# When the first tokens, the later tokens and the second block of weights are made ready at the start of a one-layer model

## The chip, the cores and the metric

The kernel runs on one core of a Trainium2 chip. The metric is device time in microseconds (us) of one execution. The profile speaks of the core's engines by short names: PE (TensorE, matrix products and transposes, with PEld for its weight loads), ACT (ScalarE), DVE (VectorE), POOL (GpSimd) and SP (SyncE, which issues most transfers). Each engine works through its own list of instructions in order.

## The reference

The reference is one layer of a hybrid model for 512 tokens of width 1024, in float32. It has a token mixer, an attention to a memory of 256 rows, and a mixture of 32 experts, each followed by a layer norm. Only the start of the token mixer matters here:

```
proj = h @ w_in                       # 512 x 1024 by 1024 x 8744
g_q, g_k, g_v, g_z, g_b, g_a, ... = split(proj)
qkv = silu(causal_dwconv(concat(g_q, g_k, g_v), conv_w))    # 4 taps
beta = sigmoid(g_b)
g = -exp(a_log) * softplus(g_a + dt_bias)
```

`g_z`, `g_b` and `g_a` lie side by side in `w_in`. `g` and `beta` are the gates of a delta rule that runs over chunks of 64 tokens. All outputs are needed in nearly float32 precision.

## The kernel before, in words

**Products in three parts.** A float32 operand is split into a high part (rounded, made by ACT) and a low part (the rest, made by DVE, from the high part); this is `split`, lines 137 to 139, and the text calls it *parting*. A product is then three matrix products (`mm3`, lines 222 to 224): weights high by tokens high, low, and crosswise. Both the tokens and every block of weights have to be parted first.

**Tokens.** `x` comes in four tiles of 128 tokens (t = 0 to 3, line 162). Since the products need tokens with the width on the partitions, `part(t)` (line 258) transposes a tile on PE in two groups of four (line 228) and parts each group out of PSUM.

**Blocks.** The wide product with `w_in` is cut into blocks of 256 or 260 columns. `dense` (line 179) goes through a list of them: it fetches the next block's raw weights as the present block begins, and writes the parting of the next block's weights into the program once a share `PART` (0.35) of the present block's estimated time is written. The first block is `z3` (line 335, columns of `g_z`, `g_b` and `g_a`): for each tile t it makes 24 products of 260 columns into a PSUM tile `mm`, DVE copies the gate columns out (`ab`, line 343), ACT takes a tanh (line 347) and DVE multiplies (`zl`, line 348). PSUM has two `mm` tiles, so a new group of products waits until the last reader of the group two before it, which is the line-348 step here, is done. The second block is called k00 here and the third k01: the key columns of heads 0 and 1, and of heads 2 and 3. Each is 48 products of 512 columns in two halves (c0 and c1), and after each half come a convolution (ACT line 432, three DVE steps of line 435), a tanh (ACT line 438), a multiplication (DVE line 439), and transposes on PE (line 228) that ACT copies out and squares (lines 469 and 471). The raw weights of k00 are parted in two pieces, those of k01 in one.

**Gates and sines.** After `z3`, `token_gates` (line 368) works out the gates in some twenty small DVE steps, up to `gg` (line 386), which PE then sums (lines 388 and 389). `rotary_sines` (line 295) takes two sines on ACT, which need another table of functions than tanh and exp do; `ACT_TABLE_LOAD` in the profile is such a change of tables.

**What sets the order.** A scheduling layer takes the program as written and lays down, ahead of time, a fixed order for each engine; buffers and waits follow from it. `tc.issue_after(i)` holds the instructions written in its block behind instruction i on i's engine. SP's order is that of the fetches.

Of the kernel before, what the change touches and what calls it, by code (L numbers as in the profile page):

```python
# [32 lines left out]
NT = S // 128  # L33
# [3 lines left out]
G_Q, G_K, G_V, G_Z, G_B = 0, 1024, 2048, 3072, 4096  # L37
N_Q, C_K, C_V, S_K, S_V, W_K, W_V, N_G, M_G = 4112, 5136, 5392, 5648, 5904, 6160, 6416, 6672, 6696
NBLK = 31
WB = 260  # L40
# [44 lines left out]
def body(tc, I, O, dbg=None):  # L85
    nc = tc.nc
    ctx = ExitStack()
    with ctx:
        _body(ctx, tc, nc, I, O, dbg or {})


def _body(ctx, tc, nc, I, O, dbg):
# [28 lines left out]
    def B8(shape, dt=FT):  # L121
        return big.tile(shape, dt, name="b8", bufs=NB8)

    def t512(shape, dt=FT):
        return wk.tile(shape, dt, name="t512", bufs=6)
# [5 lines left out]
    def rows_of(pr):  # L131
        return lambda t: pr[t // 2][:, t % 2]
# [4 lines left out]
    def split(hi, lo, src, eng=V):  # L137
        A.activation(hi, src, AF.Copy)  # L138
        eng.tensor_tensor(lo, src, hi.bitcast(FT), op=OP.subtract)  # L139

    def fetch_w(src, c0, n, loads=1):
        raw = B8([128, KD, WB])
        for k in pieces(loads):
            nc.sync.dma_start(raw[:, k, :n], src[128 * k.start:128 * k.stop, c0:c0 + n].rearrange("(k p) c -> p k c", p=128))
        return raw

    def load_w(src, c0, n, eng=V, loads=1, splits=1):
        return part_w(fetch_w(src, c0, n, loads), n, eng, splits)

    def part_w(raw, n, eng=V, splits=1):  # L150
        hi = B8([128, KD, WB], FR)
        lo = B8([128, KD, WB], FR)
        for k in pieces(splits):
            split(hi[:, k, :n], lo[:, k, :n], raw[:, k, :n], eng)
        return hi, lo

    def pieces(m):
        return [slice(KD // m * i, KD // m * (i + 1)) for i in range(m)]

    xn = [B8([128, 2, D]) for _ in range(2)]  # L160
    for t in range(NT):
        nc.sync.dma_start(xn[t // 2][:, t % 2], x_in[128 * t:128 * t + 128])
        if t == 0:
            first = load_w(I["w_in"][0], G_Z + 3 * WB, WB, loads=4, splits=4)

    bfm = ep.tile([128, 5, 128], BF, name="bfm")
    msk = t512([128, 512])
# [11 lines left out]
    def dense(blocks, cur=None):  # L179


        for j, b in enumerate(blocks):
            nb = blocks[j + 1] if j + 1 < len(blocks) else None
            raw, nxt, done = nb and fetch_w(*nb[1:4]), None, 0.0
            for us in b[4](*cur):
                yield us
                done += us
                if nb and nxt is None and done > PART * (5.3 if b[0][0] == "x" else 10.4):
                    nxt = part_w(raw, nb[3], splits=SPL.get(nb[0], 1))
            if nb and nxt is None:  # L190
                nxt = part_w(raw, nb[3])
            yield b[0]
            cur = nxt
# [26 lines left out]
    def mm3(out, wh, wl, xh, xl, first=True, last=True):  # L220

        T.matmul(out, wh, xh, start=first, stop=False)  # L222
        T.matmul(out, wh, xl, start=False, stop=False)  # L223
        T.matmul(out, wl, xh, start=False, stop=last)  # L224
# [29 lines left out]
    def parts_T(src):  # L254

        sh, sl = ([B8([128, 4, S], FR) for _ in range(2)] for _ in range(2))

        def part(t):
            for q in range(2):
                p = ps.tile([128, 512], FT, name="tp")  # L260
                transposes(p, [src(t)[:, (4 * q + i) * 128:(4 * q + i + 1) * 128] for i in range(4)])
                pv = p.rearrange("p (a b) -> p a b", a=4)
                split(sh[q][:, :, t * 128:(t + 1) * 128], sl[q][:, :, t * 128:(t + 1) * 128], pv)
        return sh, sl, part


    xh, xl, part = parts_T(rows_of(xn))
    for t in range(NT):
        part(t)


    ropec = ep.tile([128, S], FT, name="ropec")
# [2 lines left out]
    def before(engine):  # L275

        return [i for i in nc.cur_bb.bb.instructions if i.engine == engine][-1]
# [30 lines left out]
    p = ps.tile([128, 512], FT, name="tp")  # L308
# [5 lines left out]
    w_in = I["w_in"][0]  # L314

    def proj_tok(hi, lo, n, t, out):
        for k in range(KD):
            yield n * 3 / 2400
            mm3(out, xh[k // 4][:, k % 4, t * 128:(t + 1) * 128], xl[k // 4][:, k % 4, t * 128:(t + 1) * 128],
                hi[:, k, :n], lo[:, k, :n], first=k == 0, last=k == KD - 1)  # L320
# [14 lines left out]
    def z_block(j):  # L335

        def emit(hi, lo):
            n = WB if j < 3 else WB - 16
            for t in range(NT):
                p = ps.tile([128, 512], FT, name="mm")  # L340
                yield from proj_tok(hi, lo, WB, t, p[:, :WB])
                if j == 3:
                    V.tensor_copy(ab[:, t], p[:, n:WB])
                c = slice(WB * j, WB * j + n)
                zt = zl[:, t] if j == 3 else t512([128, WB])
                th = t512([128, WB])
                A.activation(th[:, :n], p[:, :n], AF.Tanh, scale=0.5)
                V.scalar_tensor_tensor(zt[:, :n], th[:, :n], 1.0, p[:, :n], op0=OP.add, op1=OP.mult)
                if j < 3:
                    m_ = rows_of(merged)(t)[:, c]  # L350
                    V.tensor_tensor(m_, m_, zt[:, :n], op=OP.mult)
        return ("z%d" % j, w_in, G_Z + WB * j, WB, emit)
# [698 lines left out]
    blocks += [{"m": m_block, "z": z_block}[b[0]](int(b[1])) for b in GATES]  # L1051
    blocks += [mem_block(j) for j in range(XB)] + [q_block(j) for j in range(4)] + [mem_block(j) for j in range(XB, 8)]
    W = Weave(dense(blocks, first))
    rotary()
    W.until("z3")
# [55 lines left out]
    for t in range(NT):  # L1111
        P = PP[t][:, 0].rearrange("p (a b) -> p a b", a=4)
        PT = PP[t][:, 1].rearrange("p (a b) -> p a b", a=8)
        for q in range(2):
            p = ps.tile([128, 512], FT, name="tp")
# [323 lines left out]
    def gate_up(pr, prev=None, last=False):  # L1439

        q, pp = pr // 2, pr % 2
        if not pp:
            rest = gather(q)
        xg = quads[q][0]
        if pr == 2:
            gb8.append(load_gb())
        load_next(6)
        ph = ps.tile([128, 512], FT, name="ga", bufs=4)
        hT = None
        for k in range(KD):  # L1450
            if pr == 0 and k == 4:
                rest()
            if prev is not None and k == (KB_LAST if last else KBACK):
                hT = swiglu(prev)
            if last and k == KD_LAST:
                down(pr - 1, hT)
            for i in range(2):
                T.matmul(ph[64 * i:64 * i + 64], xg[:, k, 128 * pp + 64 * i:128 * pp + 64 * i + 64],  # L1458
                         WT[2 * pr + i, k // 4][:, :, k % 4], start=k == 0, stop=k == KD - 1)
        if not pp:  # L1460
            if q == 0:
                weights()
            places(q)
        return ph, hT
# [21 lines left out]
    for pr in range(NE // 2 - 1):  # L1486
        last = pr == NE // 2 - 2
        nxt = gate_up(pr + 1, cur[0], last)
# [122 lines left out]
    with tc.If(most > CAP):  # L1611
# [5 lines left out]
        for t in range(NT):  # L1617
            for q in range(2):
                p = ps.tile([128, 512], FT, name="tp")
# [31 lines left out]
PART = 0.35  # L1651
# [22 lines left out]
```

## Time and profile before

| | us |
|---|---|
| median of 3 runs | 1229.37 (1223.86 to 1233.8) |
| the profiled execution, as timed | 1230.37 |
| its span, first to last instruction | 1228.4 |
| PE busy | 1162.4, 95% of the span |
| DVE busy | 655.3, 53% |
| ACT busy | 458.2, 37% |
| POOL busy | 133.6, 11% |
| mean granted clock of TensorE | 0.967 of full speed |

Times in the profile count from the start of the span. "Busy" is time in which an engine executes something. A row of the timeline gives when an instruction began, how long it took, and in brackets how long its engine had stood idle before it and what ended that wait. The chain of waits of this profile covers only the last two steps of the kernel and says nothing about the start, so the start has to be read from the timeline.

### The profile page before, as it was taken

The page shows a single profiled execution, that of the slowest core. Times are in us where ns is not written, and L with a number is a line of the kernel's source. Part 1 is how long each engine was busy: PE and PEld are TensorE (multiplying, and loading weights), DVE is VectorE, ACT ScalarE, POOL GpSimd, SP SyncE. Part 2 cuts the span into 40 slices and gives each one's busy share as a digit, 9 for nine tenths or more (in the row PEclk, how much of TensorE's full clock was granted, in tenths as well). Part 3 has the DMA queues.
Part 4 walks back from the last instruction along what each step waited for, and adds up shares of the span by engine and source line. Part 5 has one row for each costly group of instructions (what it writes and reads, how often), then busy time and mean ns, then how long its engine had stood idle before and what let it go on. Part 6 is the DMA issues. An engine that isn't in the chain of part 4 may idle for free. (4 is left out here: it accounts for less than half of the span.)

```text
span 1228.4 us, 20788 instructions
## 1 busy us (share of the span) xinstructions
PE 1162.4 (95%) x8356; PEld 926.7 (75%) x8356; DVE 655.3 (53%) x1667; ACT 458.2 (37%) x1093; POOL 133.6 (11%) x141
## 2 busy tenths in 40 slices
PE   6989999899999999999999899999989999999994
PEld 5887788678888789999998798889985445455532
DVE  4697377974865526556568667242583221221157
ACT  4643446444434124343356415244241111111224
POOL 4120000200000000000000101000020000000185
PEclk9998899898999999999999999999989999999997
DMA  8221112122222751212540614218447999999823
GB/s 273 69 69 37 35 35 69 35 71 69 70 69 83 236 156 59 71 36 69 206 125 14 196 52 138 66 52 293 172 172 262 329 381 371 406 398 386 318 84 130
DMA packets 101881, 189.21 MB, mean 154 GB/s; under 512 B 10246, under 2 KB 74438, under 8 KB 97680
## 3 DMA queue, kind: packets, MB, share of 16 engines
q1 hardware_dynamic: 93456, 181.58, 42.1%
q0 software_dynamic: 2224, 3.94, 1.0%
q10 hardware_dynamic: 6096, 2.27, 0.8%
q8 instruction: 68, 1.11, 0.4%
q14 instruction: 37, 0.30, 0.1%
HBM read 177.93 MB, written 13.63 MB: 156 GB/s over the span
## 5 line engine op out<-in xcount | busy, mean ns | idle before, releaser
L222 PE MATMUL mm<-b,b 128*128 128x256 f32 (+3 forms) x1216 | 403.7, 333 | 11.7 <-ACT b L138 7.7
L224 PE MATMUL mm<-b,b 128*128 128x256 f32 (+3 forms) x1216 | 392.8, 323 | 3.5 <-DVE b L139 3.5
L223 PE MATMUL mm<-b,b 128*128 128x256 f32 (+3 forms) x1216 | 392.4, 323 | 2.2 <-DVE b L139 2.2
L222 PEld LDWEIGHTS mm<-b,b 128*128 128x128 f32 x1216 | 232.6, 192 | 33.7 <-ACT b L138 8.5
L224 PEld LDWEIGHTS mm<-b,b 128*128 128x128 f32 x1216 | 232.7, 191 | 25.1 <-DVE b L139 4.2
L223 PEld LDWEIGHTS mm<-b,b 128*128 128x128 f32 x1216 | 233.2, 192 | 19.2 <-DVE b L139 3.0
L139 DVE TENSOR_TENSOR b<-b,b 128x2048 fp32r<-128x2048 f32 (+4 forms) x58 | 124.7, 2151 | 53.8 <-ACT b L138 43.6
L1458 PE MATMUL ga<-b,b 128*64 128x512 f32 x512 | 131.5, 608 | 6.8 <-DVE b L1345 6.8
L138 ACT ACTIVATE b<-b 128x2048 fp32r<-128x2048 f32 (+4 forms) x58 | 104.4, 1800 | 23.0 <-DMA b<-in_w_in_dram 5.8
L1458 PEld LDWEIGHTS ga<-b,b 128*64 128x64 f32 x512 | 38.4, 138 | 73.8 <-issue 63.2
L228 PE MATMUL tp<-cs,b 128*128 128x128 f32 x376 | 59.4, 285 | 11.1 <-DMA cs<-in_cst_dram 5.8
L435 DVE SCALAR_TENSOR_TENSOR t<-mm,cw,t 128x511 f32<-128x511 f32 (+2 forms) x72 | 53.7, 746 | 26.7 <-ACT t L432 25.4
L1473 PE MATMUL ga<-b,t 128*64 128x512 f32 x256 | 63.9, 593 | 0.5 <-ACT t L1317 0.5
L1338 PE MATMUL mm<-t,b 128*128 128x256 f32 x240 | 61.5, 294 | 0.0
L1310 DVE SCALAR_TENSOR_TENSOR t<-t,ga 128x256 f32<-128x256 f32 x16 | 6.7, 419 | 98.4 <-ACT t L1309 98.4
L228 PEld LDWEIGHTS tp<-cs,b 128*128 128x128 f32 x376 | 44.6, 146 | 17.6 <-DMA cs<-in_cst_dram 5.8
L1338 PEld LDWEIGHTS mm<-t,b 128*128 128x128 f32 x240 | 48.8, 204 | 0.8 <-issue 0.8
L1473 PEld LDWEIGHTS ga<-b,t 128*64 128x64 f32 x256 | 20.0, 137 | 36.2 <-issue 35.1
L1317 ACT ACTIVATE t<-tp 128x256 f32<-128x256 f32 x16 | 6.1, 383 | 88.8 <-PE tp L228 88.8
L826 POOL MEMSET b<- 128x97 f32 x32 | 5.4, 179 | 308.7 <-PE ga L773 204.3
L1321 POOL DMA_INDIRECT ybuf<-b,idx x14 | 13.7, 980 | 215.3 <-ACT b L1481 111.2
L1337 PE MATMUL mm<-t,hh 128*128 128x256 f32 x120 | 34.9, 311 | 0.0
(441 smaller groups left out, 1781.9 us busy)
## 6 DMA issues: line engine op xcount, KB each, us to landing
b<-in_moe_w_gate_dram SPq DMA_DIRECT2D x64, 512.0 KB, 10.6
b<-in_moe_w_up_dram SPq DMA_DIRECT2D x64, 512.0 KB, 10.4
b<-in_moe_w_down_dram SPq DMA_DIRECT2D x32, 1024.0 KB, 12.5
b<-in_w_in_dram SPq DMA_DIRECT2D x22, 1024.0 KB, 5.3
b<-in_w_in_dram SPq DMA_DIRECT2D x10, 1040.0 KB, 5.2
b<-in_cmp_w_dram SPq DMA_DIRECT2D x16, 512.0 KB, 7.4
b<-in_xa_wkv_dram SPq DMA_DIRECT2D x8, 1024.0 KB, 5.4
ybuf<-t SPq DMA_DIRECT2D x1, 4096.0 KB, 17.2
```

What stands on the lines that cost most here:

```text
L138: A.activation(hi, src, AF.Copy)
L139: eng.tensor_tensor(lo, src, hi.bitcast(FT), op=OP.subtract)
L222: T.matmul(out, wh, xh, start=first, stop=False)
L223: T.matmul(out, wh, xl, start=False, stop=False)
L224: T.matmul(out, wl, xh, start=False, stop=last)
L228: T.transpose(dst_psum[:, i * 128:(i + 1) * 128], s_, ident)
L435: V.scalar_tensor_tensor(acc[:, s_:], pp[:, :S - s_], cw[:, c_:c_ + 1], acc[:, s_:], op0=OP.mult, op1=OP.add)
L1321: G.indirect_dma_start(out=ybuf[:, :], out_offset=bass.IndirectOffsetOnAxis(ap=idx, axis=0), in_=yt, in_offset=None, bounds_check=2 * S - ...
L1337: T.matmul(p, rows_of(hh)(t)[:, c], sv, start=t == 0, stop=False)
L1338: T.matmul(p, rows_of(hl)(t)[:, c], sv, start=False, stop=t == NT - 1)
L1458: T.matmul(ph[64 * i:64 * i + 64], xg[:, k, 128 * pp + 64 * i:128 * pp + 64 * i + 64], WT[2 * pr + i, k // 4][:, :, k % 4], start=k == 0, ...
L1473: T.matmul(py[64 * i:64 * i + 64], hT[:, k, 64 * i:64 * i + 64], WT[2 * pr + i, 2][:, k, 512 * n:512 * n + 512], start=k == 0, stop=k == 1)
```

## The change

Four edits, all at the start of the program:

- the first block's raw weights are fetched at the same place as before, but parted later, after `part(0)`;
- only tile 0 of the tokens is transposed and parted ahead of block `z3`;
- `part(1)`, `part(2)` and `part(3)` are written inside `z3`, each after 15 of the 24 products of the tile before it (i counts the eight triples), and held behind the product written last on PE;
- within the first block alone, the parting of the second block's weights is written at a share of 0.8 of its time and not at 0.35.

```diff
     for t in range(NT):
         nc.sync.dma_start(xn[t // 2][:, t % 2], x_in[128 * t:128 * t + 128])
         if t == 0:
-            first = load_w(I["w_in"][0], G_Z + 3 * WB, WB, loads=4, splits=4)
+            first = fetch_w(I["w_in"][0], G_Z + 3 * WB, WB, loads=4)
...
-                if nb and nxt is None and done > PART * (5.3 if b[0][0] == "x" else 10.4):
+                if nb and nxt is None and done > (PART if j else 0.8) * (5.3 if b[0][0] == "x" else 10.4):
                     nxt = part_w(raw, nb[3], splits=SPL.get(nb[0], 1))
...
     xh, xl, part = parts_T(rows_of(xn))
-    for t in range(NT):
-        part(t)
+
+
+    part(0)
+    first = part_w(first, WB, splits=4)
...
                 p = ps.tile([128, 512], FT, name="mm")
-                yield from proj_tok(hi, lo, WB, t, p[:, :WB])
+                for i, us in enumerate(proj_tok(hi, lo, WB, t, p[:, :WB])):
+                    if j == 3 and i == 5 and t < NT - 1:
+                        with tc.issue_after(before(mybir.EngineType.PE)):
+                            part(t + 1)
+                    yield us
```

The changed file has two more lines from line 268 on, and six more from line 347 on, so that line 432 of before is line 438 there, 438 is 444 and so on. The text uses the numbers of before unless it says otherwise. SP's and POOL's orders are the same in both programs. On PE, ACT and DVE the order differs up to about an eighth of PE's list; behind that the three are the same.

**ScalarE, from its first parting into `z3`.** `b_83` are the first block's raw weights, `tp` a group of transposed tokens, `b_209` the raw weights of k00. Before:

```order
L138 ACTIVATE b_88<-b_83 128x520 x3
L138 ACTIVATE b_108<-tp 128x4x128
L138 ACTIVATE b_88<-b_83 128x520
L138 ACTIVATE b_109<-tp 128x4x128
L138 ACTIVATE b_108<-tp 128x4x128
L138 ACTIVATE b_109<-tp 128x4x128
L138 ACTIVATE b_108<-tp 128x4x128
L138 ACTIVATE b_109<-tp 128x4x128
L138 ACTIVATE b_108<-tp 128x4x128
L347 ACTIVATE t_237<-mm 128x244
L138 ACTIVATE b_109<-tp 128x4x128
L138 ACTIVATE b_250<-b_209 128x4x256
```

All four tiles of tokens stood ahead of the first piece of k00's weights. In the changed program, the same stretch (the raw weights of k00 are called `b_167` there):

```order
L138 ACTIVATE b_98<-tp 128x4x128
L138 ACTIVATE b_99<-tp 128x4x128
L138 ACTIVATE b_116<-b_83 128x520 x4
L313 ACTIVATE cw<-tp 128x96
L138 ACTIVATE b_98<-tp 128x4x128
L138 ACTIVATE b_99<-tp 128x4x128
L353 ACTIVATE t_209<-mm 128x244
L138 ACTIVATE b_302<-b_167 128x4x256
L138 ACTIVATE b_98<-tp 128x4x128
L138 ACTIVATE b_99<-tp 128x4x128
L138 ACTIVATE b_302<-b_167 128x4x256
```

The first tokens stand ahead of the first weights, and the first piece of k00's weights stands ahead of the tokens of tile 2, the second piece ahead of those of tile 3.

**VectorE, at the end of `z3`.** `b_375` are the raw weights of k01, and the `zl` steps are those that free an `mm` tile. Before:

```order
L139 TENSOR_TENSOR b_251<-b_209,b_250 128x4x256 x2
L343 COPY ab<-mm 128x16
L348 SCALAR_TENSOR_TENSOR zl<-t_272,mm 128x244
L343 COPY ab<-mm 128x16
L348 SCALAR_TENSOR_TENSOR zl<-t_301,mm 128x244
L343 COPY ab<-mm 128x16
L139 TENSOR_TENSOR b_396<-b_375,b_395 128x8x256
L348 SCALAR_TENSOR_TENSOR zl<-t_330,mm 128x244
```

In the changed program:

```order
L354 SCALAR_TENSOR_TENSOR zl<-t_252,mm 128x244
L139 TENSOR_TENSOR b_100<-tp,b_98 128x4x128
L139 TENSOR_TENSOR b_101<-tp,b_99 128x4x128
L349 COPY ab<-mm 128x16
L139 TENSOR_TENSOR b_396<-b_375,b_395 128x8x256
L354 SCALAR_TENSOR_TENSOR zl<-t_295,mm 128x244
L349 COPY ab<-mm 128x16
L377 TENSOR_TENSOR gx<-ab,rowb 128x32
L379 TENSOR_SCALAR gu<-gx 128x32
L354 SCALAR_TENSOR_TENSOR zl<-t_330,mm 128x244
```

The low parts of k01 now stand ahead of the `zl` step of tile 2, and no longer only ahead of that of tile 3. ACT's order has the same turn: k01's high parts stand ahead of the tanh of tile 2. Behind these rows the gates' steps run to `gg` without a convolution step between them; before, three line-435 steps and one line-439 step of k00 stood among them. On PE the sum of the gates (lines 388 and 389) stands behind 24 products of k00, where it stood behind 45.

**ScalarE, around the two sines.** `t_408` is the convolution of k00's half c0, `t_455` that of c1. Before:

```order
L432 ACTIVATE t_408<-mm,cw 128x512
L438 ACTIVATE t_413<-t_408 128x512
L393 ACTIVATE egc<-gcum 128x32
L392 ACTIVATE egl<-tp 128x32
L469 ACTIVATE b_378<-tp 128x512
L396 ACTIVATE ekd<-ekd 128x32
L297 ACT_TABLE_LOAD
L297 ACTIVATE ropec<-ropes 128x512
L471 ACTIVATE sq,sst<-tp 128x128
L298 ACTIVATE ropes<-ropes 128x512
```

In the changed program:

```order
L438 ACTIVATE t_408<-mm,cw 128x512
L398 ACTIVATE egl<-tp 128x32
L399 ACTIVATE egc<-gcum 128x32
L402 ACTIVATE ekd<-ekd 128x32
L299 ACT_TABLE_LOAD
L299 ACTIVATE ropec<-ropes 128x512
L444 ACT_TABLE_LOAD
L444 ACTIVATE t_413<-t_408 128x512
L300 ACT_TABLE_LOAD
L300 ACTIVATE ropes<-ropes 128x512
L475 ACTIVATE b_378<-tp 128x512
```

The tanh of c0 (line 438 before, 444 now) has gone from ahead of the first sine to between the two, and the tables are loaded five times in the whole program and not three times.

## Rows read from the trace of the kernel before

**Rows 1.** The page: its first line, and busy time (share) and instructions of each engine.

```profile
span 1228.4 us, 20788 instructions
PE 1162.4 (95%) x8356; PEld 926.7 (75%) x8356; DVE 655.3 (53%) x1667; ACT 458.2 (37%) x1093; POOL 133.6 (11%) x141
```

**Rows 2.** Busy time by window: length, PE, PEld, DVE, ACT, POOL, clock, DMA share, GB/s.

```profile
17.20:82.00 64.80, 64.73 (x460) 59.78 (x459) 47.56 (x113) 38.45 (x103) 13.24 (x12) 1.00 0.33 103
```

**Rows 3.** Timeline of the start: begin, length, engine, line [idle before, what ended it].

```profile
7.93 0.21 ACT L368 ACTIVATE ea<-rowb 128x8 f32<-128x8 f32 x1 [4.42 <-DMA rowb<-in_gdn_a_log_dram]
...
12.29 0.58 ACT L138 ACTIVATE b<-tp 128x512 fp32r<-128x512 f32 x1
...
12.92 0.59 PE L222 MATMUL mm<-b,b 128*128 128x260 f32 x1 [5.20 <-ACT b L138]
```

**Rows 4.** Timeline of SP's issues: the later tiles of x, then the blocks.

```profile
5.73 2.69 SPq L162 DMA_DIRECT2D b<-in_x_dram  x3
8.46 78.34 SPq L144 DMA_DIRECT2D b<-in_w_in_dram  x8
```

**Rows 5.** Issues from 5.5 to 6.5, and at 8.5: count, KB, us to landing.

```profile
b<-in_x_dram SPq DMA_DIRECT2D x2, 512.0 KB, 9.0
...
b<-in_w_in_dram SPq DMA_DIRECT2D x1, 1024.0 KB, 10.9
```

**Rows 6.** Timeline of PE: transposes, products of the first block, then of k00.

```profile
18.12 0.60 PE L228 MATMUL tp<-cs,b 128*128 128x128 f32 x4
...
22.29 0.37 PE L222 MATMUL mm<-b,b 128*128 128x260 f32 x1
...
29.80 0.28 PE L224 MATMUL mm<-b,b 128*128 128x260 f32 x1
29.92 0.39 PE L222 MATMUL mm<-b,b 128*128 128x512 f32 x1
...
40.10 0.40 PE L224 MATMUL mm<-b,b 128*128 128x512 f32 x1
```

**Rows 7.** Timeline: k01's high and low parts, and the last zl step.

```profile
27.78 1.91 ACT L138 ACTIVATE b<-b 128x2048 fp32r<-128x2048 f32 x1
...
30.21 2.28 DVE L139 TENSOR_TENSOR b<-b,b 128x2048 fp32r<-128x2048 f32 x1
32.41 0.40 DVE L348 SCALAR_TENSOR_TENSOR zl<-t,mm 128x244 f32<-128x244 f32 x1
```

**Rows 8.** Timeline: the gates on DVE, and PE's sum of them.

```profile
32.81 0.18 DVE L371 TENSOR_TENSOR gx<-ab,rowb 128x32 f32<-128x32 f32 x1
...
36.66 0.74 DVE L435 SCALAR_TENSOR_TENSOR t<-mm,cw,t 128x511 f32<-128x511 f32 x1
37.32 0.18 DVE L382 TENSOR_TENSOR gp<-gp,gu 128x32 f32<-128x32 f32 x1
...
40.33 0.18 DVE L386 SCALAR_TENSOR_TENSOR gg<-gp,ea 128x32 f32<-128x32 f32 x1
...
40.57 0.41 PE L388 MATMUL tp<-gg,cs 128*128 128x32 f32 x2
```

**Rows 9.** Timeline of ACT: k00's first tanh, table and sine, a copy, a tanh.

```profile
39.06 0.63 ACT L438 ACTIVATE t<-t 128x512 f32<-128x512 f32 x1 [2.61 <-DVE gp L382]
...
42.44 1.28 ACT L297 ACT_TABLE_LOAD   x1
43.73 0.63 ACT L297 ACTIVATE ropec<-ropes 128x512 f32<-128x512 f32 x1
...
52.70 0.60 ACT L469 ACTIVATE b<-tp 128x512 f32<-128x512 f32 x1 [0.16 <-PE tp L228]
...
54.19 0.66 ACT L438 ACTIVATE t<-t 128x512 f32<-128x512 f32 x1
```

**Rows 10.** Timeline: the longest wait of PE up to 100 us, and ACT before it.

```profile
86.44 0.38 ACT L728 ACTIVATE b<-mm 128x256 f32<-128x256 f32 x1 [2.47 <-PE mm L224]
...
89.97 0.80 PE L224 MATMUL mm<-b,b 128*128 128x512 f32 x1 [3.11 <-DVE b L139]
```

**Rows 11.** A short wait of PE among the experts, and the window after it (columns as in 2).

```profile
986.76 1.97 PE L1458 MATMUL ga<-b,b 128*64 128x512 f32 x2 [1.14 <-DVE b L1345]
...
986.70:990.10 3.40, 3.34 (x8) 1.74 (x9) 0.45 (x2) 0.33 (x1) 0.65 (x1) 0.50 1.03 411
```

## The prediction

> **What bounds the kernel now.** I read the page first: PE is busy for 95% of the span [rows 1], so time is won where PE stands idle and lost where it has to stand. The only long idle time that the change can reach is at the start. The timeline shows it [rows 3]: ScalarE takes up its first work at 7.93 us, the parts of the first tokens only at 12.29, and PE's first product comes at 12.92, let go by ScalarE. The windows then show that from 17.2 to 82 us PE is busy for 64.73 of 64.80 us [rows 2]. So the change works between a stretch in which PE waits for data and a stretch in which it has practically no wait. Whatever wait the new order puts into the second stretch is lost in full; that is where I look hardest. The transfers set the fixed points, because SP's order is not changed: the second tile of x lands at 5.73 + 9.0 = 14.7, and the raw weights of k00 at 8.46 + 10.9 = 19.4 [rows 4, 5].
>
> **The head start.** ScalarE can make the first tokens' parts from 7.93 + 0.21 = 8.1 on, about four us sooner, and the products of tile 0 start as soon as the first piece of weights is parted, between 9.8 at best (8.1, two parts and a piece at about 0.6 each) and 12.9 at worst. I count nothing for the transpose of the convolution weights, which now stands ahead of the first product: its cover is the next limit. That limit is the second tile of x. Its transposes now stand among the products of tile 0, behind 15 of 24, and it lands at 14.7.
>
> From there PE goes on with two groups of transposes (at most 0.60 each [rows 6]), nine products of tile 0 and fifteen of tile 1. A product takes 0.121 (22.29 to 29.80 is 62 steps [rows 6]). That brings it to 18.8, two more groups to 20.0, nine more products to 21.1, where tile 2's products should follow.
>
> **First stall, 1.3 us.** On ScalarE the first half of k00's parting now stands ahead of tile 2's parts, and its data land at 19.4. A half takes about 0.95 on ScalarE and 1.15 on VectorE (half of 1.91 and of 2.28 [rows 7]). So VectorE is through with its half at 19.4 + 0.95 + 0.05 + 1.15, about 21.6, and with the low part of tile 2's first group, about 0.7 later, at 22.3 to 22.4. The third product of tile 2 needs that part. At 22.29 the old order had 63 products to go and no transposes; the new one has at 22.4 some 46 products and two groups to go, 5.6 + 1.2 = 6.8 us, which is 29.2 against 29.92 [rows 6]. Of the head start of up to three us, 0.7 is left.
>
> **Second stall: k00 begins 0.4 late.** PE has two `mm` tiles, so the first product of k00 waits for the `zl` step of tile 2. That step used to come early; now it stands on VectorE behind the low parts of k01, and they behind the high parts on ScalarE, which stand behind tile 3's parts. In order: tile 3's first group is transposed at 22.4 + 13 x 0.121 + 0.6 = 24.6, its two parts take ScalarE to about 25.7, k01's high parts 1.91 to 27.6, the low parts 2.28 to 29.9, the `zl` step 0.40 to 30.3 [rows 7]. Against 29.92 that is 0.4 late, whatever PE has gained before.
>
> **Third: the gates, 0.4.** The gates' first step follows at about 30.4. Before, they took from 32.81 to 40.51. Four convolution steps of k00 stood among them, each of which put the next small step back by about 0.55 (36.66 to 37.32, where small steps follow 0.1 to 0.2 apart [rows 8]); these 2.2 go, and a `zl` step and a small one come in, 0.6. That makes 7.7 - 2.2 + 0.6 = 6.1, so `gg` is there at 36.5. PE now reaches the gates' sum behind 24 products of k00, at 30.3 + 24 x 0.231 = 35.85 (the 0.231 is 29.92 to 40.10 over 44 steps [rows 6]): it stands for 0.65. Before it stood from 40.33 to 40.57, 0.24 [rows 8].
>
> **Fourth: two more table loads, 1.05 and 1.5.** Before, the tanh of k00's c0 ran at 39.06, ahead of table load and sine at 42.44 and 43.73 [rows 9], and PE found its transposes ready. Now the convolution steps stand behind the gates, and the tanh between the sines. From the sum at 36.55: sum 0.41, four small steps and one convolution step on VectorE 1.46, a small step on ScalarE 0.2 and hand-overs 0.2 lead to 38.85; then load 1.28, sine 0.63, load 1.28, tanh 0.63 to 42.7; multiplication 0.7 to 43.4. PE is through with its other 23 products at 42.35 and stands for 1.05. For c1 the same again: after 42.7 come a load, the second sine, a copy with four squares (52.70 to 54.19, 1.5 [rows 9]), the convolution with 0.7 and its three steps of 0.76, a load, the tanh and the multiplication: 51.6. PE has 26 products of k01 in hand from 44.05 to 50.05, so it stands for 1.55; I take 1.5. Their bounds: nothing, if the loads run while ScalarE waits anyway; and 1.28 more each, if a load costs twice its row.
>
> The Trainium skill, page "ScalarE: Activation LUTs", section "What ACT_TABLE_LOAD costs", speaks against this order: a switch costs the load of 1.28 us and a drain of about 1.4, and the page's rules say to finish one set before going to the next. The trace agrees with the load; the drain it doesn't show, since the sine starts 1.29 after the load began. With the page's figure, as an estimate, the sum would be some 4 us higher.
>
> **The sum.** 0.4 + 0.4 + 1.05 + 1.5 = 3.35 us later when k01 is done. From there PE's order is the old one but for single steps, and I expect the lag to be carried to the end. The longest later wait up to 100 us, 3.11 at 89.97 [rows 10], doesn't soak it up: it is for weights whose parting stood on ScalarE behind a step that itself waited for PE at 86.44, so it moves along. The profiled execution took 1230.37 and would take 1233.7; the median shown is 1.0 lower, so I predict 1232.7. By about one per cent, 12 us, can a measurement of this kernel be told from no change; this is a quarter of that.
>
> **The rivals.**
> - *The head start survives* (0.22). If k00's weights land sooner or the steps behind it find slack, PE runs on from 14.7 with 81 products and six groups, 9.8 + at most 3.6, and ends the first block at 28.1, 1.8 ahead; at most 12.92 - 9.8 = 3.1 ahead. For it: ScalarE does become free early. Against it: three fixed points in a row, each behind the other. It gives 1226.5 to 1227.5, say 1227.
> - *The clock falls in the new waits* (0.14). Among the experts PE waited 1.14 us at 986.76, and the granted clock of the 3.4 us that follow is 0.50, the lower of the two levels, 1.2 GHz [rows 11]; that costs 1.7. From 17.2 to 82 it stood at 1.00 throughout, without waits [rows 2]. The new order has four waits of about 1.1 to 1.5 us there. One fall is within the forecast's own spread; with two or more this case decides, and with all four it is 3.35 + 6.8 later, 1239.5.
> - *The lag is soaked up* (0.12): VectorE, not PE, sets the pace of the delta rule's stages, and a late PE only waits less. Against it is the wait at 89.97, above. It gives the old time, 1229.4.
> - *A table switch costs more than its load row* (0.04). If the three loads on the two ways above cost double, 3.8 more: 1236.5. The row speaks against it, for the sine follows at once. This is the page's case in the trace's numbers.
>
> **How the numbers follow.** The forecast has 0.48, with 1231 to 1235 as its own range. The range reaches from the surviving head start to most of the clock's case, 1225 to 1240, and leaves out under two in ten. To be faster by over 1% the time would have to be under 1217.1, which no case gives: 0.02 for what I have not seen. Slower by over 1% is over 1241.7, past four clock falls: 0.05. Within 1%: 0.93.
>
> **What would show it.** Right: the first product at about 10.5, a wait of PE ahead of tile 2's third product, k00's first product at about 30.3 with VectorE's `zl` step as what let it go, and waits of PE for the two transposes of k00 between 43 and 52, with five table loads on ScalarE. Wrong: k00's first product ahead of 29, or no wait at those transposes. The sum is also wrong if the products of k01 end less than two us later than before, or if a later wait of PE is shorter by the lag.

## The result, and the profile after

The changed kernel takes 1237.49 us (median of 20 runs, 1229.71 to 1242.76), the kernel before 1229.97 us in the same comparison (20 runs, 1221.97 to 1237.15). The ratio is 1.0064 [1.0047, 1.0081]: 5.8 to 10.0 us slower. That is no change by the measure of one per cent, and it lies in the stated range of 1225 to 1240. It lies outside the 1231 to 1235 that the forecast had for itself, at twice the forecast lag of 3.35 us. The profiled execution took 1237.31 us.

**The start.** Rows of the timeline, in the columns of [rows 3]:

```profile
8.56 0.58 ACT L138 ACTIVATE b<-tp 128x512 fp32r<-128x512 f32 x1
...
10.12 0.39 PE L311 MATMUL tp<-cs,cwn 96*128 96x96 f32 x1 [2.43 <-DMA cwn<-in_gdn_conv_w_dram]
...
10.22 0.57 PE L222 MATMUL mm<-b,b 128*128 128x260 f32 x1
...
21.32 0.39 PE L222 MATMUL mm<-b,b 128*128 128x260 f32 x1 [1.08 <-ACT b L138]
...
22.69 0.39 PE L224 MATMUL mm<-b,b 128*128 128x260 f32 x1 [0.87 <-DVE b L139]
...
27.91 2.29 DVE L139 TENSOR_TENSOR b<-b,b 128x2048 fp32r<-128x2048 f32 x1 [0.92 <-ACT b L138]
29.09 0.28 PE L224 MATMUL mm<-b,b 128*128 128x260 f32 x1
30.12 0.40 DVE L354 SCALAR_TENSOR_TENSOR zl<-t,mm 128x244 f32<-128x244 f32 x1
...
30.67 0.47 PE L222 MATMUL mm<-b,b 128*128 128x512 f32 x1 [1.30 <-DVE ab L349]
```

The first product comes 2.70 us sooner than before. By 22.69 two waits have taken 1.95 us of it, and k00 begins at 30.67, 0.75 later than before [rows 6]. What its product waits for is the `zl` step of tile 2, which stands behind k01's low parts and ends at 30.52; the row names `ab`, the small copy that follows `zl` on VectorE.

```profile
36.38 0.19 DVE L392 SCALAR_TENSOR_TENSOR gg<-gp,ea 128x32 f32<-128x32 f32 x1
...
36.63 0.41 PE L394 MATMUL tp<-gg,cs 128*128 128x32 f32 x2
...
40.65 1.28 ACT L444 ACT_TABLE_LOAD   x1
41.94 0.63 ACT L444 ACTIVATE t<-t 128x512 f32<-128x512 f32 x1
42.59 1.28 ACT L300 ACT_TABLE_LOAD   x1
...
43.36 0.65 PE L228 MATMUL tp<-cs,b 128*128 128x128 f32 x4 [0.67 <-DVE b L445]
...
49.11 1.28 ACT L444 ACT_TABLE_LOAD   x1 [2.50 <-DVE t L441]
...
51.81 0.44 PE L228 MATMUL tp<-cs,b 128*128 128x128 f32 x2 [1.53 <-DVE b L445]
...
60.00 0.36 PE L222 MATMUL mm<-b,b 128*128 128x256 f32 x1
...
93.40 0.80 PE L224 MATMUL mm<-b,b 128*128 128x512 f32 x1 [3.04 <-DVE b L139]
```

The tanh of k00 stands between the sines, with a table load ahead of it and one behind it, and PE waits for both transposes of k00. The row at 60.00 is the first product behind k01; in the kernel before it is this one:

```profile
56.30 0.36 PE L222 MATMUL mm<-b,b 128*128 128x256 f32 x1
```

So the lag at the end of k01 is 3.70 us, and at the wait of [rows 10] it is 93.40 - 89.97 = 3.43 us.

**The rest, by stages.** The windows give for each stretch its length, PE's busy time, the granted clock, the share of the DMA engines and what they moved. The changed kernel:

```profile
17.20:82.00 64.80, 59.21 (x405) 1.00 0.31 98
82.00:112.00 30.00, 26.96 (x141) 0.89 0.16 49
112.00:140.00 28.00, 26.11 (x605) 0.82 0.26 78
140.00:850.00 710.00, 694.89 (x5201) 0.98 0.29 93
850.00:940.00 90.00, 83.12 (x620) 0.92 0.54 194
940.00:1140.00 200.00, 192.39 (x1013) 0.95 0.97 367
```

The kernel before, behind the stretch of [rows 2]:

```profile
82.00:112.00 30.00, 26.89 (x247) 0.89 0.12 37
112.00:140.00 28.00, 26.12 (x493) 0.82 0.25 76
140.00:850.00 710.00, 694.59 (x5200) 0.98 0.30 94
850.00:940.00 90.00, 82.91 (x617) 0.94 0.55 197
940.00:1140.00 200.00, 192.40 (x1024) 0.97 0.98 375
```

PE stands for 5.6 us between 17.2 and 82 where it stood for 0.07. Behind that these stretches differ in the clock alone: 0.92 for 0.94 and 0.95 for 0.97 at the experts. Read by themselves they say: 3.4 us early, and some 4 us of half clock among the experts. That was my first theory, and it did not hold.

### The profile page after: what moved, and what is told of

The parts are those of the page before. It is cut to its first block, busy times and chain, and to the rows that moved or that the text cites. A ratio compares the mean times of both kernels' runs of the same rounds, so it can differ in the third digit from the quotient of the medians.

```text
span 1235.4 us, 20789 instructions
## 1 busy us (share of the span) xinstructions
PE 1167.3 (94%) x8356; PEld 932.2 (75%) x8356; DVE 656.0 (53%) x1667; ACT 460.8 (37%) x1095; POOL 135.1 (11%) x141
## 5 line engine op out<-in xcount | busy, mean ns | idle before, releaser
L1344 PE MATMUL mm<-t,b 128*128 128x256 f32 x240 | 65.5, 307 | 0.0
L1344 PEld LDWEIGHTS mm<-t,b 128*128 128x128 f32 x240 | 51.9, 216 | 0.8 <-issue 0.8
```

The source lines that it names most:

```text
L1344: T.matmul(p, rows_of(hl)(t)[:, c], sv, start=False, stop=t == NT - 1)
```

## The experiments

Theory A: the change costs the early lag, and what lies above it is the clock. Theory B: the rest is work or waits of the change. In the texts that were written ahead of the runs, A1 puts the clock's part at 120 us, A2 at the experts, and A3 at any wait beside small products. Below, "mean" and "clock" are the mean time and the mean granted clock of all runs of a kernel; each comparison also has 32 to 35 runs of the kernel before, and their clocks.

| kernel | runs | mean us | mean clock | ratio to before, interval |
|---|---|---|---|---|
| before, all three comparisons | 102 | 1229.2 | 0.9688 | |
| the change | 20 | 1237.4 | 0.9640 | 1.0064 [1.0047, 1.0081] |
| before_again | 12 | 1227.4 | 0.9702 | 0.9997 [0.9971, 1.0023] |
| sines_behind_k00 | 12 | 1233.0 | 0.9684 | 1.0028 [1.0002, 1.0054] |
| fill_before | 12 | 1230.9 | 0.9742 | 1.0017 [0.9988, 1.0046] |
| fill_after | 9 | 1237.6 | 0.9716 | 1.0067 [1.0035, 1.0098] |
| fill120_after | 12 | 1232.0 | 0.9698 | 1.0021 [0.9997, 1.0046] |
| fill90_120_after | 12 | 1231.8 | 0.9717 | 1.0014 [0.9990, 1.0038] |
| fill90_120_before | 12 | 1230.3 | 0.9708 | 1.0003 [0.9976, 1.0030] |
| fillC_after | 12 | 1231.6 | 0.9716 | 1.0022 [0.9994, 1.0049] |
| hold120_after | 12 | 1232.8 | 0.9688 | 1.0029 [0.9998, 1.0059] |
| four_pieces | 12 | 1231.4 | 0.9685 | 1.0014 [0.9991, 1.0037] |
| best | 12 | 1228.2 | 0.9765 | 0.9989 [0.9965, 1.0013] |
| best_before | 12 | 1223.4 | 0.9788 | 0.9950 [0.9928, 0.9973] |

### The kernel before once more

> The kernel before once more, for the mean granted clock of each of its runs (of the first runs only their times are known). The changed kernel's 20 runs lie on a line: 1193.4 us plus 1222 us times the share of the clock that is missing, with a mean clock of 0.964 and a mean time of 1237.4. Theory A (the change costs about 3.3 us in the first 60 us, and the rest of the 7.5 us are additional stretches at half clock among the experts): these runs lie on a line of nearly the same slope some 3.3 us lower, and their mean clock is higher by about 0.0033 (4 us). Theory B (the rest is work or waits of the change that have nothing to do with the clock): the mean clock is again 0.964 and the line lies some 7.5 us lower. The time itself should be 1230, ratio 1.000.

The 102 runs of the kernel before lie on a line too: 1194.8 us and 1103 us times the missing share of the clock. At the changed kernel's 0.9640 it gives 1194.8 + 1103 x 0.0360 = 1234.5, and the changed kernel took 1237.4. So at equal clock the change costs 2.9 us, about the early lag, and the lower clock (0.0048 x 1103) costs 5.3: theory A. The changed kernel was not run a second time, and for the 20 runs beside it no clock of the kernel before is on record; by the line, their mean of 1229.9 us belongs to 0.968. The 12 runs of this kernel alone had a higher clock still.

But its profile, against theory A as I had placed it:

```profile
82.00:112.00 30.00, 26.92 (x347) 1.00 0.22 70
112.00:140.00 28.00, 26.84 (x475) 1.00 0.13 41
940.00:1140.00 200.00, 192.39 (x1009) 0.95 0.97 367
```

The same program as in [rows 1] has the full clock from 82 to 140 us here, where the first profile has 0.89 and 0.82, and the half clock behind all six waits among the experts, as the changed kernel has. This execution is 3.87 us shorter all the same. One pair of profiles does not tell which stretches at half clock belong to the change. The Trainium skill, "TensorE: Matmul & The Clock Gate", Part 1, tells of such differences between runs of one kernel for its first products; here they lie at 82 to 140 us and among the experts.

### The sines behind k00

```diff
     token_gates()
+    W.until("k00")
     rotary_sines()
     W.until("k01")
```

> The changed kernel with the two sines written behind block k00, so that ScalarE has three table loads at the start and not five. By the terms of my sum (1.05 + 1.5 us for PE's waits for the two transposes of k00) the products of k01 end 2.5 to 2.8 us sooner than in the changed kernel, within 1 us of the kernel before, and both waits are gone. For the whole: 1237.4 - 2.7 = 1234.7 if the stretches at half clock among the experts stay as many (theory A, 1231 to 1236); if a late start is what brings more of them about, it goes back to 1230. Rival: the waits for the transposes were covered later anyway, and the time stays at 1237.4 in spite of the earlier end of k01.

The terms for the tables were right: both waits are gone, and the first product behind k01 comes at 57.25, 2.75 us sooner than in the changed kernel. But the gain is lost at the next wait, which is 1.1 us longer:

```profile
93.28 0.79 PE L224 MATMUL mm<-b,b 128*128 128x512 f32 x1 [4.15 <-DVE b L139]
```

93.28 against 93.40: the lag at 90 us is what it was. The rows say where the gain went. In this program the two sines, with their table loads, stand on ScalarE among k01's steps, ahead of the tanh of k01's first half, and the transposes behind this tanh stand on PE behind products of the next block:

```profile
51.61 1.28 ACT L299 ACT_TABLE_LOAD   x1
...
54.65 1.28 ACT L516 ACT_TABLE_LOAD   x1
...
56.85 0.62 ACT L444 ACTIVATE t<-t 128x512 f32<-128x512 f32 x1
...
65.88 0.17 DVE L497 TENSOR_SCALAR se<-sst 128x16 f32<-128x16 f32 x1 [2.41 <-ACT sq L477]
```

This tanh comes at 56.85; it was 57.48 in the changed kernel and 54.19 in the kernel before [rows 9]. The step `se`, which waits for ScalarE's last squares of k01, opens a row of small steps on VectorE without a pause up to the parting that PE waits for at 90 us. It begins at 65.88 here, in the changed kernel and in the kernel before at these times:

```profile
65.86 0.18 DVE L497 TENSOR_SCALAR se<-sst 128x16 f32<-128x16 f32 x1 [3.15 <-ACT sq L477]
```

```profile
62.41 0.17 DVE L491 TENSOR_SCALAR se<-sst 128x16 f32<-128x16 f32 x1 [2.50 <-ACT sq L471]
```

So the gain was lost among k01's steps, ahead of VectorE's row; how much of it to the sines' new place and how much to the transposes' was not tested. And the lag at 90 us is the lag of this row: 65.86 - 62.41 = 3.45 for the change.

The mean is 4.4 us lower than the changed kernel's, with the clock back at 0.9684. At equal clock this kernel stands 3.4 us above the line of the kernel before, as a lag of 3.3 at 90 us says.

### Filling among the experts, first try

```diff
         xg = quads[q][0]
+        if not pp and q:
+            idle = ps.tile([128, 512], FT, name="tp")
+            for i in range(5):
+                T.matmul(idle, rows_of(hh)(0)[:, :128], rows_of(hh)(1)[:, :512], start=i == 0, stop=i == 4)
```

> The kernel before with five products that nothing uses (128 rows by 512 columns, about 0.23 us each) written ahead of each of seven quads of experts from the second on, between the gather's last product and PE's wait of 1.14 us; the output is unchanged. They fill the wait, they don't make it longer. Theory A (PE's 1.14-us waits among the experts lead to the stretches of 3.4 us at half clock, each some 1.5 us dear): those stretches are gone, four of the six in the profile, so 1230 - 6 = 1224 (1222 to 1226), with the clock up by 0.004 to 0.005. Rival (the stretches come from the many small products and transposes ahead of the wait, or from something beside PE's idleness): as many stretches as before, and 1230 or up to 1 us more.

> The same fill in the changed kernel, where all six waits of 1.14 us were followed by a stretch at half clock. Theory A: 6 x 1.5 = 9 us less, 1228.4 (1226 to 1231), and the distance to the filled kernel before is the early lag alone, 3 to 4.5 us (4.5 if the stretch at 867 us, which another wait brings, stays). Theory B (the changed kernel's other 4 us have nothing to do with the clock): the two filled kernels differ by 7 to 8 us, as the unfilled ones do. Rival (fill has no effect on the clock): 1237 to 1238.

Both missed their aim (1224 and 1228 expected, 1230.9 and 1237.6 measured). What frees the waiting product stands on VectorE behind steps that need the small products, so the filling pushed the wait along and cost its own time, 7 x 1.17 = 8.2 us. The wait is still there in the filled changed kernel:

```profile
PE ga L1468 <- DVE b L1351: 6.8, 6, 1.1
```

That is six waits of together 6.8 us. The half clock came less often all the same, behind two of the six in either profile (four and six without filling). Gain and cost cancelled. The two filled kernels still differ by 6.7 us in the mean, which alone would speak for theory B; but their clocks differ too, and at equal clock they stand 7.7 and 11.4 us above the line: 3.7 apart, the early lag.

### Filling at 120 us and at 90 us

At 120 us the fixed order of the changed kernel differs from that of before, which the prediction had passed over. PE in the kernel before (line 571 and 575 are small products of the delta rule, line 228 transposes):

```
L571 MATMUL ga<-b_797 32x32 x64
L575 MATMUL ga<-b_797 32x32 x46
L228 MATMUL tp<-cs,b_958 128x128 x4
L575 MATMUL ga<-b_797 32x32 x18
```

In the changed kernel the transposes stand eight rows of such a listing further on, since on VectorE a parting of 2.3 us has come ahead of the multiplication that they wait for:

```
L577 MATMUL ga<-b_797 32x32 x64
L581 MATMUL ga<-b_797 32x32 x64
L224 MATMUL mm<-b_98,b_982 128x512
```

PE's waits there, in the kernel before and in the changed one:

```profile
117.17 0.66 PE L228 MATMUL tp<-cs,b 128*128 128x128 f32 x4 [0.88 <-DVE b L439]
...
119.14 0.31 PE L575 MATMUL ga<-b 32*32 32x32 f32 x12 [0.99 <-issue]
```

```profile
121.58 0.26 PE L581 MATMUL ga<-b 32*32 32x32 f32 x7 [1.89 <-issue]
```

In these two profiles, two waits of up to a microsecond have become one of 1.89. The experiments fill it, and the wait at 90 us; `idle(n, lo, hi)` writes n products of `lo` by `hi` into a PSUM tile that nothing reads:

```diff
+                if hf == 0 and which == "q" and i == 0:          # at 90 us
+                    idle(13, hi[:, 0, :128], xh[0][:, 0])
...
             for b in B32:
                 T.matmul(p2[b, u], pb[b, u], XTC[b, u], start=True, stop=True)
+            if hf == 0 and u == 12:                              # at 120 us
+                idle(11, xh[0][:, 0, :128], xh[0][:, 0], "ga", bufs=4)
```

> The changed kernel with eleven products that nothing uses (128 rows by 512 columns, 0.23 us each) written into the delta rule's small products at about 120 us, where PE waited 1.9 us in one piece (0.9 and 0.3 to 1.0 in the kernel before) and 10.2 us at half clock followed in two of two profiles. Theory A1 (that wait brings the half clock, and with it about 4 of the 7.5 us): no stretch at half clock between 115 and 135, the mean clock of the runs 0.967 or 0.968 for 0.964, and 1237.4 - 4.5 + at most 1 for the filling = 1233 to 1234. Rival A2 (the clock among the experts makes the difference, this place does not): 1237 to 1238, mean clock up by at most 0.001.

> As fill120_after, and thirteen such products ahead of the wait of 3.0 us for parted weights at 90 us, which 6.8 or 3.4 us at half clock followed in all three profiles of the changed kernel's order and in two of three of the order before. Theory A1: both stretches go, together 14 to 17 us at half clock, some 7 us of time: 1230 to 1231, mean clock 0.970. Rival A2: 1237 to 1238.

> The same two fillings in the kernel before; its order at 120 us becomes that of the changed kernel. With the clock undisturbed up to 220 us in both, only the lag of the first 60 us should be left between this kernel and fill90_120_after: 3.0 to 3.5 us (theory A1), so 1227 here, against 7.5 (theory B: the rest of the loss is not the clock's) or 1 and less (if the early lag is covered later).

With the filling at 120 us alone the mean is 1232.0 for 1237.4 and the clock 0.9698 for 0.9640. That is what A1 says, but it does not prove A1: sines_behind_k00 above, and hold120_after and four_pieces below, keep the long wait and its half clock in their profiles, and their clocks are 0.9684 to 0.9688 and their means 1231.4 to 1233.0, which cannot be told from this kernel's. In this profile the long wait is gone, and the stretch has the full clock:

```profile
112.00:140.00 28.00, 27.67 (x537) 1.00 0.25 78
```

The filling at 90 us raised the clock by another 0.002 and gave no time that can be told (1231.8). In the kernel before the two fillings gave nothing either: 1230.3, where 1227 was expected. The two fully filled kernels differ by 1.4 us in the mean, with intervals of 3 us each: that alone can't tell 3.4 from 1. At equal clock it is 2.4.

### Filling among the experts, behind the small products

```diff
+        if q:
+            idle(5, rows_of(hh)(0)[:, :128], rows_of(hh)(1)[:, :512])
         if q < NQ - 1:
             quads[q].append(B8([128, 2, D]))
             return
```

> The changed kernel with five unused products in each of PE's waits of 1.14 us among the experts, this time behind the small products, directly ahead of the product that waits (the first filling stood ahead of the small products and only pushed the wait back: PE still waited 1.14 us each time). If these waits lead to the stretches of 3.4 us at half clock: the six or seven stretches between 940 and 1140 are gone, the waits too, 6 x 1.4 = 8 us less, 1229 (1228 to 1231), mean clock 0.972. If the small products in front of the wait lead to them: as many stretches as before, 1237.

```profile
940.00:1140.00 200.00, 199.21 (x1082) 1.00 0.99 381
```

No half clock is left between 940 and 1140 us, and PE's six waits there are filled. The first of the products that waited and the last transposes, in the changed kernel and in this one:

```profile
958.07 1.07 PE L1464 MATMUL ga<-b,b 128*64 128x512 f32 x2 [1.14 <-DVE b L1351]
...
1216.17 1.02 PE L1531 MATMUL tp<-b,b 128*128 128x512 f32 x2
```

```profile
958.87 1.07 PE L1471 MATMUL ga<-b,b 128*64 128x512 f32 x2
...
1209.57 1.02 PE L1538 MATMUL tp<-b,b 128*128 128x512 f32 x2
```

Between the two PE needs 1209.57 - 958.87 = 250.7 us, in the changed kernel 1216.17 - 958.07 = 258.1: 7.4 less, for 8 expected. The mean is 5.8 below the changed kernel's, at 1231.6, for 1228 to 1231 expected; this profile happened to have 0.76 between 112 and 140 us, behind a wait of 2.49.

### The order at 120 us put back

```diff
-                if nb and nxt is None and done > (PART if j else 0.8) * (5.3 if b[0][0] == "x" else 10.4):
-                    nxt = part_w(raw, nb[3], splits=SPL.get(nb[0], 1))
+                if nb and nxt is None and done > (0.6 if j == 6 else PART if j else 0.8) * (5.3 if b[0][0] == "x" else 10.4):
+                    with tc.issue_after(done_silu[-1]) if j == 6 else ExitStack():
+                        nxt = part_w(raw, nb[3], splits=SPL.get(nb[0], 1))
...
         V.scalar_tensor_tensor(out, th, 1.0, acc, op0=OP.add, op1=OP.mult)
+        done_silu.append(before(mybir.EngineType.DVE))
```

> The changed kernel with one parting written later and held behind the multiplication of the half before it, so that at 120 us the order is again like that of the kernel before: on VectorE the multiplication ahead of the parting, on PE the four transposes inside the small products and not behind them. If the new order at this place is what brings the half clock (A1): PE waits there in two pieces and not 1.9 us in one, a stretch at half clock follows in fewer of the executions, and the time is 1233 to 1235. If any wait beside the small products brings it (A3): 10 us at half clock at 120 as in the changed kernel, 1237.

The time is about what A1 said (1232.8, clock 0.9688), but its reason is not: the transposes stand inside the small products again, and PE's long wait is still there, now within them:

```profile
118.71 0.33 PE L231 MATMUL tp<-cs,b 128*128 128x128 f32 x1 [0.53 <-DVE b L448]
120.91 0.90 PE L231 MATMUL tp<-cs,b 128*128 128x128 f32 x3 [1.86 <-issue]
```

with the half clock behind it (0.88 from 112 to 140). So, in this profile, the place of the transposes does not make the wait.

### The early terms taken away, and the best version

```diff
+    W.until("k00")
     rotary_sines()
...
-SPL = {"k00": 2}
+SPL = {"k00": 4, "k01": 4}
```

`best` adds the three fillings to this, `best_before` adds them to the kernel before.

> The changed kernel with the early terms taken away: the sines behind block k00, and the raw weights of k00 and k01 parted in four pieces each, so that tile 2's multiplication stands between k01's pieces on VectorE; the transposes at 120 us stand inside the small products again. By my sum PE is then ahead of the kernel before, by 0.4 to 1.1 us at the end of the first third's half (it was 2.8 to 3.3 us behind): first product of k00 at 28.2 to 28.8 us and no waits for the transposes of k00. The time: 1237.4 - 3.9 = 1233.5 if the clock stays as in the changed kernel, 1229 if the stretch at 120 us goes as well (theory A: 1229 to 1234). Rival: the early lag is not what is carried, 1237.

> All of it together: four_pieces with the three fillings (at 90 us, at 120 us, and in the six waits of 1.14 us among the experts). From the changed kernel: 3.9 us of early lag, 5.5 us at 120 us and 0.2 at 90 us as measured, 5.9 us among the experts as measured: 1237.4 - 15.5 = 1222 (1218 to 1225), mean clock 0.977 or more, faster than both kernels. If the parts do not add (because the clock falls elsewhere instead): 1227 to 1231.

> The kernel before with the same three fillings, to see what of the best version comes from the change: 1230.3 (with the two early fillings) - 6 to 8 among the experts = 1223. If the mended head start is worth its 0.4 to 1.1 us, the best version is faster than this by that, which is about what a comparison can tell.

four_pieces has the expected time, 1231.4, but its profile not the expected start. PE waited 1.75 us in the first block, and the clock fell behind that wait; the window has PE's columns, as above:

```profile
23.62 0.48 PE L224 MATMUL mm<-b,b 128*128 128x260 f32 x1 [1.75 <-DVE b L139]
```

```profile
24.00:26.00 2.00, 2.00 (x11) 0.50 1.12 365
```

Its first product of k00 came at 31.65, for 28.2 to 28.8 expected, and the products of k01 ended 1.85 us behind the kernel before. In the profile of `best`, which has the same start and kept the full clock there, its wait ended 0.42 us sooner and they were at 29.71 and 0.13 us ahead. So the fall cost about 31.65 - 29.71 - 0.42 = 1.5 us. It is no single case: of the nine profiles with the changed start, two (four_pieces and fill_after) have the half clock between 24 and 28 us; of the five with the order before, none has.

At 90 us the wait of four_pieces is 4.17 us. ScalarE and VectorE on these weights:

```profile
83.45 1.91 ACT L138 ACTIVATE b<-b 128x2048 fp32r<-128x2048 f32 x1
```

```profile
91.83 2.28 DVE L139 TENSOR_TENSOR b<-b,b 128x2048 fp32r<-128x2048 f32 x1
```

The high parts were ready at 85.36, and VectorE took up the low parts 6.5 us later, behind its unbroken row of small steps of the delta rule's inverse. In the kernel before, the parting of the same weights began on ScalarE at 81.01 and on VectorE at 87.63: there too VectorE sets this wait. The sines stand among k01's steps here as in sines_behind_k00, and `se` begins at 66.75 (64.80 in `best`, 62.41 before). So this version does not tell what a lead of PE would be worth if the sines stood elsewhere.

best_before is the fastest, 0.9950 [0.9928, 0.9973], as expected; best, with the mended change, is not (0.9989), 4.8 us behind it, where 1222 was expected. The parts did not add. Its PE waits 1.94 us at 90 us in spite of the filling, where best_before has no wait, and it shows 0.88 from 112 to 140 us behind a wait of 2.21, where best_before has 1.00. So the change has no share in the gain.

## Why the prediction was right and wrong

- *Head start*: right. First product 10.22 for 10.5. The transpose of the convolution weights, counted at nothing, stood ahead of it with a wait for its transfer that ended 0.10 us before the first product.
- *First stall*: it came 0.9 us sooner and was longer, 1.08 and 0.87 for 1.3, but it ended as forecast, since the data end it. The last product of `z3` began at 29.09; its successor could have followed at 29.2, as forecast.
- *k00 late*: 0.75 for 0.4. `zl` ended at 30.52 for 30.3, and the product followed 0.15 later.
- *Gates*: `gg` at 36.4 for 36.5, as worked out. But PE, having begun k00 later, stood only 0.31 for the sum, against 0.24 before: 0.07 for 0.4.
- *Two more table loads*: 0.67 and 1.53 for 1.05 and 1.5. With the sines moved both waits were gone and the end of k01 came 2.75 us sooner, so the term was shown by taking it away. The Trainium skill, "ScalarE: Activation LUTs", section "What ACT_TABLE_LOAD costs", adds a drain of about 1.4 us to each load; the trace disagrees once more, the tanh began 1.29 us after its load.
- *The sum*: 3.35 forecast; 3.70 at the end of k01, 3.43 at 90 us, and 2.9 at equal clock over all runs. The first product behind k01 lies between 55.97 and 57.39 in the five profiles with the order before, on average at 56.5, and between 59.64 and 60.00 in the five with the changed start that kept the full clock and their sines in place, on average at 59.8: 3.3. The terms above make 3.0; the rest up to the end of k01 lies between these waits and is not itemised. That the sum came so close is partly luck: k00 was sized too low and the gates too high, by a third of a microsecond each.
- *Carried to the end*: right for this lag, but not for the reason given. The prediction took ScalarE's parting at 86.72, behind the step at 86.44, for the one that PE waits for at 89.97. It is that of the weights after these; the high parts that PE waited with were ready at 82.92. What carries the lag is VectorE's row of small steps from `se` on, 3.45 us later. To that extent the rival "the lag is soaked up" was right that VectorE sets the pace there; but VectorE itself was late.
- *The step that failed*: the clock, sized at nothing outside of 17 to 82 us, in "From there PE's order is the old one but for single steps". The runs showed a mean clock of 0.9640 for 0.9688, worth 5.3 us by the line. One of the single steps, at 120 us, stands beside a wait of 1.89 us in place of two short ones, but the runs do not show that this place makes the difference. The rival with the clock had the right resource. Its place was wrong in the first profile, which stayed at 1.00 from 17 to 82 us in spite of its waits, and right in two of nine profiles with this start. Its price of 1.7 us for one fall [rows 11] was too high among the experts, 7.4 us for six or 1.2 each, and nearer at the start, 1.5.
- *The range*: the time lies in it because the range reached into the clock's case, not because the forecast case came about.

**What is shown and what is not.** Shown: the lag of about 3 us, by rows and at equal clock; that the changed kernel's 20 runs have a clock lower by 0.0048; that unused products in PE's waits among the experts end the half clock there and save 7.4 us in that stretch.

Not shown: where the changed kernel's lower clock comes from. For the place at 120 us speak the profiles without a filling there. In the three of the order before, the longest wait at this place is 0.9 to 1.0 us, with the half clock in one of them; in the six with the changed start it is 1.7 to 2.5 us, with the half clock in all six. Against it speak two things. On average these profiles miss 4.2 us of clock between 112 and 140 us with the changed start and 1.7 in the order before; that is 2.5 us of the 5.9 that 0.0048 of the span would be, an estimate from few profiles. And three variants that keep the long wait (sines_behind_k00, hold120_after, four_pieces) have the clock of the kernel before all the same. It may be that several places share in it, the first block among them, or that the 20 runs were low for a reason that the variants' runs did not have: the changed kernel was not run again beside them. Why the wait at 120 us is longer is open too; hold120_after speaks against the transposes' place.

## What to carry to other kernels

When a change moves PE by some microseconds, the price has two parts: the lag, which the rows of the first stages give well, and the clock, which one profile before and one after do not give, since the stretches at half clock vary between executions of one program. Plot the time of every run against its mean clock and compare the lines before looking for a mechanism in one pair of traces. When a variant brings the time back, look whether variants that leave the suspected place alone bring it back as well; here three did. And a short wait of PE may be worth more than its length: unused products in the waits of the unchanged kernel gained 0.5%. The head start of 2.7 us, in contrast, was gone by the first block's end, to waits for parted data. What moving the two sines gave back was gone before VectorE's long row began, which waits for ScalarE: after moving a step, follow every engine to its next wait, not only the one that was relieved.

## What the runs showed of the hardware

- A wait of 1.14 us of PE behind small products was followed by a stretch at half clock (1.2 of 2.4 GHz) in four of six cases in one profile of the kernel before and in six of six in another; with five products in its place, in none of six; with five more products ahead of it and the wait left as it was, in two of six.
- Among the delta rule's products of 32x32, PE waited for something that the profile does not show ("issue"). In three profiles of the order before it waited 0.99, 0.28 and 0.59 us at the same place; with other orders up to 2.7. Over all 14 profiles, the half clock followed in seven of the eight whose longest wait at this place was 1.7 us or more, and in one of the six where it was 1.2 or less. After the longest, 2.66 in best_before, the clock stayed full: the wait alone does not decide it.
- Two waits of PE in the first block, together 2.4 us in fill_after, and one of 1.75 us in four_pieces, were followed by a stretch at half clock (granted clock 0.50 from 24 to 26 us in four_pieces); waits of together 1.0 to 1.95 us at the same place in seven other profiles were not.
